# FFN 1's second GEMM on one core: difference operands and four low parts built by adding transfers, norm vectors loaded at unit 10

## The chip, the core and the metric

The kernel runs on one core of a Trainium2 chip. The metric is the device time of one execution in microseconds. Five engines work from queues of their own: PE (TensorE) multiplies, DVE (VectorE) and ACT (ScalarE) do elementwise work, POOL (GpSimd) does elementwise work and issues transfers that can add into their destination, SP (SyncE) issues plain transfers. Each queue is worked off in program order.

## The reference

One layer of a streaming encoder on 512 tokens of width 1024, all in float32. Shortened:

```
h = x + 0.5 * post1(SwiGLU_1(pre1(x)))          # FFN 1
u = pre_mix(h)                                  # RMS norm
q, k, v, xr, xg = split(u @ w_in)
...                                             # recurrent branch, attention branch, gates, w_o
h = h + post_mix(merged @ w_o)
y = h + 0.5 * post2(SwiGLU_2(pre2(h)))          # FFN 2
SwiGLU(x) = (silu(x @ w1) * (x @ w3)) @ w2      # w1, w3: 1024 x 2816, w2: 2816 x 1024
```

The change touches `@ w2` of FFN 1 (called `w2a`), the post norm and the next norm behind it, and the first products with the columns of `w_in` that are called `xr`.

## The kernel before

Every float32 operand is split in two parts of a shorter format: a high part (`whi`, a copy on ACT) and a low part (`wlo`, source minus high part). A product is three matmuls, high by high, low by high and high by low. The low part is made in one of three ways: by DVE (a subtraction; `split_to` at L179, `prep` at L649), or by an *adding transfer*: ACT writes the negative of the high part (or of the source, rounded) into the low tile, and POOL issues a transfer that adds the source onto it (`split_dma` L161, L644, L647). The low parts in the set `BY_DMA` and the products in `by_add` take the second way.

All large tiles, weights, halves and temporaries, share one ring of 42 slots (`slot`). An instruction that writes a new tile waits until the last user of the tile that held the slot before is done.

The 22 row tiles of `w2a` are multiplied in two ways. Two tiles, the *tail* (2 and 3), are multiplied plainly (`classical`, L242 to L244). The other 20 are taken in five groups (`G` = 5) by a scheme of seven products instead of eight on half tiles b11, b12, b21, b22 of 128 x 2 x 512 (`Halves`). The products come in the order m1, m5, m2, m6, m3, m7, m4, each over the five groups: 35 *units*, unit u being product u // 5 of group u % 5. m1 reads b11; m5 reads T1 = b12 - b11, which stands in b12's tile; m2 reads T2 = b22 - T1; m6 and m7 and so on read further differences or raw halves.

- `load` (L571) fetches the raw halves on SP; `prep` (L624) makes the high and low parts of one unit's weights and of its activations (`hx`, later a part of `uT`) and then, in `sums`, the differences that later units need (`T` at L582 for weights, `S` at L585 for activations), all on DVE.
- `step(u)` (L691) first preps up to unit u + 4 (`LEAD` = 5), then runs the hooks of u, then issues the 12 matmuls of unit u. So in each engine's queue a unit's preparation stands some five units ahead of its matmuls.
- `blocks` (L701) sets hooks: the tail's transfers at units 17 and 18, its split at 21 and 22, the four tiles of x (`h_back`, L711) at 20, 22, 27 and 29. The products w1, w3 before it (`pairs_a.run`) carry `late` calls: the first four units are prepped inside its last job.
- `tok_gemm` (L364) runs units 0 to 24, the tail's products for tokens 0 to 255, preps up to unit 32 (`pre.prep(5 * G + LEAD + 3)`), queues `norm(0)`, runs m7 (units 25 to 29), the tail's products for the other tokens' second half, preps the rest, queues `norm(1)`, and runs m4 twice, for one block of 128 tokens each.
- m7's sums are added out of PSUM by DVE (`out`, L682) before m4 may add into the same banks. The hooks of units 28 and 29 split the first two tiles of `xr`.
- `norm(t)` (L316) is a chain on DVE and ACT in turn: add the parts (L294), squares (L296), root, the new h (L308), squares again (L320), and the normed block hg (L331, L332). It reads two vectors spread over 128 partitions, which `vectors` (L402) loads on POOL at unit 22 (`GPOST_AT`); POOL multiplies the second one by a constant (L404). PE then transposes hg (L341), and `mm_feat` (L224 to L226) multiplies by `xr`.

Of the kernel before, what the change touches and what calls it, by code (L numbers as in the profile page):

```python
# [51 lines left out]
def hybrid_layer(ctx: ExitStack, tc: tile.TileContext, a: dict, out: bass.AP):  # L52
# [311 lines left out]
    def tok_gemm(nm, xs, n, R, gpost_name, scale, gpre_name, first, x_to=None, xf=None, spill=False, then=None, eps=None, pre=None):  # L364

        F = n - R
        acc = {}  # L370
        w = {}

        def accs(t):
            if t not in acc:
                acc[t] = [bank("acc"), bank("acc")]
            return acc[t]

        x_to = x_to or (lambda k: None)
        if not pre:
            both = min(2, F)  # L380
            for k in range(both):
                x_to(k + 1)
                w[k] = get(nm, k, ahead=both - k + 1)
            for tt in ((0, 1), (2, 3)):
                for k in range(both):
                    for t in tt:
                        mm_tok(accs(t), xs[k], t, w[k], k == 0, False)
                        if t % 2:
                            point()
            for k in range(both, F):  # L390
                x_to(k + 2)
                w[k] = get(nm, k, ahead=2 + (R - 2) * (k + 1) // F)
                for t in range(NT):
                    mm_tok(accs(t), xs[k], t, w[k], k == 0, False)
                    if t % 2:
                        point()
        point(True)
        tail = list(pre.hid.seq) if pre else list(range(F, n))
        g, us, trs = [], {}, {}
        ep = lambda t: D * EPS if eps is None else eps[:, t : t + 1]  # L400

        def vectors():  # L402
            g.extend((bcast(gpost_name), bcast(gpre_name)))
            pool.tensor_scalar(out=g[1], in0=g[1], scalar1=NEWT, scalar2=None, op0=ALU.mult)  # L404

        def tails():
            for i, k in enumerate(tail):
                x_to(F + i + 1)
                w[k] = get(nm, k, ahead=max(0, len(tail) - 1 - i), rawahead=2)

        def classical(t, n_):
            for k in tail:
                new = k == tail[0] and (t > 1 and n_ == 1 if pre else k == 0)
                mm_tok(accs(t), xs[k], t, w[k], new, k == tail[-1], (n_,), bool(pre))

        def norm(t, mid=None):
            us[t] = norms(acc[t], t, g[0], scale, g[1], spill, ep(t), mid, pre and pre.part(t), (1, 0) if pre and t > 1 else (0, 1))

        if pre:
            G = pre.G  # L420
            pre.hooks[GPOST_AT].append(vectors)
            for i in range(2):
                pre.hooks[6 * G - 2 + i].append(lambda i=i: [split_to(st["get"] + i + 1), dma_to(st["get"] + i + 3)])
            for u in range(5 * G):
                pre.step(u)
            tails()
            for t in range(2):
                acc[t] = [pre.bank["bc"][t], pre.bank["bx"][t]]
                for n_ in range(2):
                    classical(t, n_)  # L430
            pre.prep(5 * G + LEAD + 3)
            norm(0)
            for u in range(5 * G, 6 * G):
                pre.step(u)
            for t in range(2, 4):
                acc[t] = [pre.bank["bu"][t - 2], bank("acc")]
                classical(t, 1)
            pre.prep(7 * G)
            norm(1)
            for t in range(2, 4):  # L440
                for u in range(6 * G, 7 * G):
                    pre.step(u, (t - 2,))
                trs[t - 2] = transpose_mm(us[t - 2])
                transpose_out(trs[t - 2], t - 2, xf if t == 2 else None)
                classical(t, 0)
                if t == 2:
                    norm(2)
            split_to(st["get"] + len(first))
            dma_to(st["split"] + 2)
            pre.hid.eo.clear()  # L450
            pre.bank.clear()
        else:
            tails()
            vectors()
            split_to(st["get"] + len(first))
            dma_to(st["split"] + 2)
            for t in range(NT):
                for n_ in range(2):
                    classical(t, n_)
                if t == NT - 1:  # L460
                    break
                if t >= 1:
                    trs[t - 1] = transpose_mm(us[t - 1])
                if t == NT - 2:
                    transpose_out(trs[t - 1], t - 1)
                norm(t)
                if t == 1:
                    transpose_out(trs[t - 1], t - 1, xf)

        t = NT - 1  # L470
        ws, bs = [], []

        def start(ks=range(KT)):
            i = len(bs)
            ws.append(get(*first[i], ahead=len(first) - 1 - i, rawahead=2))
            bs.append(bank("f"))
# [71 lines left out]
    class Halves:  # L548
# [4 lines left out]

        names = ("m1", "m5", "m2", "m6", "m3", "m7", "m4")

        def __init__(self, nm, hid, hooks, gs, by_add, in_slots):
            self.nm, self.hid, self.hooks, self.gs = nm, hid, hooks, gs
            self.by_add, self.in_slots = by_add, in_slots
            self.G = G = len(gs)
            self.loads = [(b, i) for i in range(G) for b in ("b11", "b12")] + [(b, i) for b in ("b22", "b21") for i in range(G)]  # L560
            self.again_at = self.names.index("m3") * G - 3
            self.raw, self.ops, self.loaded, self.ready = {}, {}, 0, 0
            self.bank, self.c, self.again, self.did = {}, {}, {}, set()
# [27 lines left out]
        def t1(self, i):  # L591
            if ("t", i) not in self.did:
                self.did.add(("t", i))
                self.T("b12", "b12", "b11", i)

        def s1(self, i):
            if ("s", i) not in self.did:
# [26 lines left out]
        def prep(self, n, load=True):  # L624

            G = self.G
            while self.ready < min(n, 7 * G):
# [1 line left out]
                self.ready += 1  # L629
                m, i = self.names[u // G], u % G  # L630
                if load:
                    self.load(min(4 * G, 2 * G + (u if u >= U_SLOTS else u == 3)))
                b, odd, half = self.OPERANDS[m]
                hi = slot([P, 2, 512], F32R, name="whi")
                lo = slot([P, 2, 512], F32R, name="wlo")
# [62 lines left out]
                later(0, lambda: self.out(m), 0)  # L698
            point()

    def blocks(nm, hid, pairs, late, h_src, gs, marks, by_add, in_slots):  # L701

        hooks = {u: [] for u in range(7 * len(gs))}

# [8 lines left out]
        for at_, fn in zip(marks, (lambda n: dma_to(st["get"] + n + 1), tail_tile, h_back)):  # L713
            for n, u in enumerate(at_):
                hooks[u].append(lambda n=n, fn=fn: fn(n))
        half = Halves(nm, hid, hooks, gs, by_add, in_slots)
        pairs.more = lambda n: half.load(LOAD_PAIRS[n])
        ahead = lambda: half.prep(min(half.ready + 1, U_SLOTS))
        end = len(pairs.jobs) - 1
        late[end, 1], late[end, 2 if pairs.R is None else 3] = [ahead], [ahead]  # L720
# [6 lines left out]
        else:  # L727
            late[5, 1].append(lambda: half.s1(0))
            late[9, 1].append(lambda: half.s1(1))
            late[13, 1] = [lambda: half.s1(2)]  # L730
        pairs.run(ahead, late)
        return half

# [606 lines left out]
    late[7, 2], late[8, 2] = [lambda: softplus_terms((3, 1))], [softplus_out]  # L1340

    h.clear()
    half = blocks("w2a", hid, pairs_a, late, lambda t: a["x"][t * P : (t + 1) * P, :], GS_A, MARKS_A, ADD_A, 6 * len(GS_A))
# [423 lines left out]
    late = {(0, 1): [lambda: X2.update(t4=to_uT(tn[3], 0, 1)), tn.clear]}  # L1767
    pairs_b.prep(1, 1)

    half = blocks("w2b", hid, pairs_b, late, lambda t: h_scr[t], GS_B, MARKS_B, ADD_B, 7 * len(GS_B))  # L1770
    X2 = pairs_b = None
    last_gemm("w2b", hid, half, "ffn2_post_g", 0.5)

# [19 lines left out]
GRAW_AT = (29, 30)  # L1793
TB_AT = (34, 35, 36, 37)

BY_DMA = {("wg", i) for i in range(2)}

BY_POOL = {("wg", i) for i in range(2, 8)} | {("wk", 0), ("wk", 1)}

# [1 line left out]
KEPT_AT = (15, 16), (18, 19), (19, 20)  # L1801
LEAD = 5
U_SLOTS = 4
LOAD_PAIRS = (0, 6, 8, 10)
GS_A = (4, 6), (8, 10), (12, 14), (16, 18), (0, 20)
MARKS_A = (17, 18), (21, 22), (20, 22, 27, 29)
ADD_A = {(m, i) for m in ("m6", "m7") for i in (3, 4)} | {("m4", i) for i in range(1, 5)}

TAIL_B = (20, 21)
GS_B = (0, 2), (4, 6), (8, 10), (12, 14), (16, 18)  # L1810
# [66 lines left out]
```

## Time and profile before

| | |
|---|---|
| median of three runs | 1122.27 us (1120.18 to 1122.67) |
| the profiled execution | 1119.84 us, its span 1118.1 us |
| PE busy | 1096.8 us, 98% of the span |
| DVE, ACT, POOL busy | 942.1 us (84%), 692.3 us (62%), 398.5 us (36%) |
| DMA | 158.54 MB, mean 142 GB/s |

The span runs from the first to the last instruction of the profiled execution; what lies around it is 1.7 us. A row of a timeline gives start and duration in us, the engine, the line, the operation, its output and inputs, and in brackets the idle time before it and what ended it. Two instructions of one engine overlap a little in these rows, so their distance (the pitch), not the duration, is what one more instruction costs its queue.

### The profile page before, as it was taken

How to read it: one execution, taken by the hardware profiler on the slowest of the kernel's cores; microseconds unless marked ns; L12 is line 12 of the kernel's file. 1: busy time of each engine (PE TensorE's matmuls, PEld its weight loads, DVE VectorE, ACT ScalarE, POOL GpSimd, SP SyncE). 2: the span in 40 equal slices, each digit the busy share in tenths (PEclk: the TensorE clock that was granted, in tenths of full speed). 3: DMA queues.
4: the chain of work that ended last, by engine and by line, in shares of the span. 5: the costliest groups of instructions: out<-in, count | busy, mean ns of one | idle time of the engine just before them, and what ended most of it. 6: DMA issues, size and time to landing. Idle time of an engine off the chain costs nothing.

```text
span 1118.1 us, 18008 instructions
## 1 busy us (share of the span) xinstructions
PE 1096.8 (98%) x6826; PEld 987.2 (88%) x6826; DVE 942.1 (84%) x1335; ACT 692.3 (62%) x1200; POOL 398.5 (36%) x332
## 2 busy tenths in 40 slices
PE   9999999999979899999999999999999999999997
PEld 8899999987758777899888888888999999998886
DVE  5878999899968878878677876867789989999995
ACT  7756555577676777856565665446555555567672
POOL 0144833202021522043456564110777566521000
PEclk9999999999998999999999999999999999999999
DMA  9334653577574573126422345251433233637642
GB/s 336 117 92 128 155 120 114 174 238 144 170 219 128 172 170 111 57 69 243 140 77 94 95 170 204 75 230 57 135 110 114 82 108 94 208 133 193 184 116 92
DMA packets 53782, 158.54 MB, mean 142 GB/s; under 512 B 5552, under 2 KB 7472, under 8 KB 53696
## 3 DMA queue, kind: packets, MB, share of 16 engines
q1 hardware_dynamic: 46000, 134.81, 35.2%
q0 software_dynamic: 7408, 22.07, 10.3%
q8 instruction: 53, 0.87, 0.3%
q10 hardware_dynamic: 288, 0.52, 0.2%
q14 instruction: 33, 0.27, 0.1%
HBM read 135.37 MB, written 13.62 MB: 133 GB/s over the span
## 4 chain that ended last, share of the span: by engine, by line
PE 69%; DVE 3%; ACT 1%; issue 1%; DVEq 0%; ACTq 0%
PE f L224 8%; PE f L225 8%; PE f L226 8%; PE c L785 8%; PE c L783 8%; PE c L784 8%; PE hw L670 4%; PE hw L672 4%; PE hw L671 4%; PE acc L244 1%; PE acc L243 1%; PE acc L242 1%; PE pt L1637 1%; DVE wlo L649 1%; PE s L1601 1%
## 5 line engine op out<-in xcount | busy, mean ns | idle before, releaser
L784 PE MATMUL c<-uT,wlo 128*128 128x256 f32 x516 | 146.0, 283 | 0.0
L785 PE MATMUL c<-uT,whi 128*128 128x256 f32 x516 | 146.0, 283 | 0.0
L783 PE MATMUL c<-uT,whi 128*128 128x256 f32 x516 | 146.0, 283 | 0.0
L783 PE MATMUL c<-Xh,whi 128*128 128x256 f32 x504 | 142.7, 283 | 0.0
L784 PE MATMUL c<-Xh,wlo 128*128 128x256 f32 x504 | 142.6, 283 | 0.0
L224 PE MATMUL f<-uT,whi 128*128 128x512 f32 (+1 forms) x368 | 136.4, 371 | 0.0
L225 PE MATMUL f<-uT,wlo 128*128 128x512 f32 (+1 forms) x368 | 134.8, 366 | 0.0
L226 PE MATMUL f<-uT,whi 128*128 128x512 f32 (+1 forms) x368 | 134.8, 366 | 0.0
L785 PE MATMUL c<-Xl,whi 128*128 128x256 f32 x456 | 129.1, 283 | 0.0
L214 DVE TENSOR_TENSOR wlo<-S,whi 128x1024 fp32r<-128x1024 f32 x86 | 121.0, 1407 | 5.8 <-POOL OL L1673 3.1
L213 ACT ACTIVATE whi<-S 128x1024 fp32r<-128x1024 f32 x86 | 88.5, 1054 | 30.0 <-DVE S L832 28.3
L783 PEld LDWEIGHTS c<-uT,whi 128*128 128x128 f32 x516 | 99.0, 192 | 0.2
L784 PEld LDWEIGHTS c<-uT,wlo 128*128 128x128 f32 x516 | 99.0, 192 | 0.2
L785 PEld LDWEIGHTS c<-uT,whi 128*128 128x128 f32 x516 | 99.0, 192 | 0.0
L783 PEld LDWEIGHTS c<-Xh,whi 128*128 128x128 f32 x504 | 96.8, 192 | 0.3 <-issue 0.3
L784 PEld LDWEIGHTS c<-Xh,wlo 128*128 128x128 f32 x504 | 96.8, 192 | 0.0
L672 PE MATMUL hw<-whi,uT 128*128 128x512 f32 x228 | 89.6, 393 | 0.5
L671 PE MATMUL hw<-wlo,uT 128*128 128x512 f32 x228 | 89.3, 392 | 0.6 <-DVE wlo L649 0.3
L670 PE MATMUL hw<-whi,uT 128*128 128x512 f32 x228 | 88.8, 389 | 0.0
L785 PEld LDWEIGHTS c<-Xl,whi 128*128 128x128 f32 x456 | 87.5, 192 | 0.0
L224 PEld LDWEIGHTS f<-uT,whi 128*128 128x128 f32 x368 | 69.4, 189 | 12.5 <-issue 1.7
L226 PEld LDWEIGHTS f<-uT,whi 128*128 128x128 f32 x368 | 69.4, 189 | 11.5
(433 smaller groups left out, 3178.8 us busy)
## 6 DMA issues: line engine op xcount, KB each, us to landing
raw_w2a<-in_w2a_dram SPq DMA_DIRECT2D x27, 512.0 KB, 4.6
raw_w2b<-in_w2b_dram SPq DMA_DIRECT2D x27, 512.0 KB, 4.7
raw_w1b<-in_w1b_dram SPq DMA_DIRECT2D x22, 512.0 KB, 4.2
raw_w3b<-in_w3b_dram SPq DMA_DIRECT2D x22, 512.0 KB, 4.4
raw_w3a<-in_w3a_dram SPq DMA_DIRECT2D x21, 512.0 KB, 4.4
raw_w1a<-in_w1a_dram SPq DMA_DIRECT2D x20, 512.0 KB, 4.5
raw_wg<-in_wg_dram SPq DMA_DIRECT2D x16, 512.0 KB, 3.9
h<-in_x_dram SPq DMA_DIRECT2D x8, 512.0 KB, 6.7
```

The source lines that it names most:

```text
L213: act.activation(hi, src, AF.Copy)
L214: dve.tensor_tensor(out=lo, in0=src, in1=f32(hi), op=ALU.subtract)
L224: pe.matmul(ps[:, c0:c1], wh[:, s], h_, start=k == 0 and c0 == 0, stop=False, skip_group_check=True)
L225: pe.matmul(ps[:, c0:c1], wl[:, s], h_, start=False, stop=False, skip_group_check=True)
L226: pe.matmul(ps[:, c0:c1], wh[:, s], l_, start=False, stop=k == KT - 1, skip_group_check=True)
L242: pe.matmul(acc[n], x[:, 0, c], wh[:, s], start=first, stop=False, skip_group_check=skip)
L670: pe.matmul(ps, xs[:, 0, j, c], hi[:, j, :], start=start and j == 0, stop=False, skip_group_check=True)
L671: pe.matmul(ps, xs[:, 0, j, c], lo[:, j, :], start=False, stop=False, skip_group_check=True)
L672: pe.matmul(ps, xs[:, 1, j, c], hi[:, j, :], start=False, stop=i == self.G - 1, skip_group_check=True)
L783: pe.matmul(ps, wh[:, s], xh, start=first, stop=False, skip_group_check=True)
L784: pe.matmul(ps, wl[:, s], xh, start=False, stop=False, skip_group_check=True)
L785: pe.matmul(ps, wh[:, s], xl, start=False, stop=k == 3, skip_group_check=True)
```

## The change

- T1 of FFN 1 is no longer a subtraction on DVE. b12 isn't loaded by SP; ACT writes -b11 into a tile and POOL issues a transfer that adds b12 onto it. The first three of these are called in the last job of the products before, ahead of the units' preparation; two more are put in hooks of units 0 and 1, but `sums` calls `t1` for units 3 and 4 before those hooks run, so they come there. SP's loads are five fewer, and the calls that pace them (`LOAD_A`) are adapted. One sum of activations (`s1(3)`) is called earlier.
- The two norm vectors are loaded at unit 10 in place of 22, and ACT in place of POOL multiplies one of them, at unit 20.
- Ahead of `norm(0)` one unit less is prepped (up to 31 in place of 32).
- The low parts of both tail tiles and of the first two `xr` tiles are made by adding transfers in place of DVE.
- m4 of groups 2, 3 and 4 gets its low part from DVE in place of an adding transfer.

FFN 2 calls the same classes with the old way of T1.

```
         def vectors():
             g.extend((bcast(gpost_name), bcast(gpre_name)))
-            pool.tensor_scalar(out=g[1], in0=g[1], scalar1=NEWT, scalar2=None, op0=ALU.mult)
+            if not pre:
+                pool.tensor_scalar(out=g[1], in0=g[1], scalar1=NEWT, scalar2=None, op0=ALU.mult)
...
-            pre.hooks[GPOST_AT].append(vectors)
+            pre.hooks[2 * G].append(vectors)
+            pre.hooks[4 * G].append(lambda: act.activation(g[1], g[1], AF.Copy, scale=NEWT))
...
-            pre.prep(5 * G + LEAD + 3)
+            pre.prep(5 * G + LEAD + 2)
             norm(0)
...
-            self.loads = [(b, i) for i in range(G) for b in ("b11", "b12")] + [(b, i) for b in ("b22", "b21") for i in range(G)]
+            self.loads = [(b, i) for i in range(G) for b in (("b11",) if add_t1 else ("b11", "b12"))]
+            self.first = len(self.loads)
+            self.loads += [(b, i) for b in ("b22", "b21") for i in range(G)]
...
         def t1(self, i):
             if ("t", i) not in self.did:
                 self.did.add(("t", i))
-                self.T("b12", "b12", "b11", i)
+                if self.add_t1:
+                    t = self.raw["b12", i] = slot([P, 2, 512], name=f"raw_{self.nm}")
+                    act.activation(t, self.raw["b11", i], AF.Copy, scale=-1.0)
+                    pool.dma_start(out=t, in_=self.src("b12", i), accum_op=ALU.add)
+                else:
+                    self.T("b12", "b12", "b11", i)
...
-                    self.load(min(4 * G, 2 * G + (u if u >= U_SLOTS else u == 3)))
+                    self.load(min(self.first + 2 * G, self.first + (u if u >= U_SLOTS else u == 3)))
...
             late[13, 1] = [lambda: half.s1(2)]
+            for i in (1, 2, 3):
+                late.setdefault((end, i), []).insert(0, lambda i=i: half.t1(i - 1))
+            late[end, 1].append(lambda: half.s1(3))
+            for i in (3, 4):
+                hooks[i - 3].append(lambda i=i: half.t1(i))
...
-BY_DMA = {("wg", i) for i in range(2)}
+BY_DMA = {("wg", i) for i in range(2)} | {("w2a", i) for i in (2, 3)} | {("xr", i) for i in range(2)}
...
-LOAD_PAIRS = (0, 6, 8, 10)
+LOAD_A, LOAD_B = (0, 3, 5, 5), (0, 6, 8, 10)
...
-ADD_A = {(m, i) for m in ("m6", "m7") for i in (3, 4)} | {("m4", i) for i in range(1, 5)}
+ADD_A = {(m, i) for m in ("m6", "m7") for i in (3, 4)} | {("m4", 1)}
```

More of the change, by code (lines that the diff above doesn't have):

```diff
@@ L554, in hybrid_layer, with __init__ @@
         names = ("m1", "m5", "m2", "m6", "m3", "m7", "m4")
-        def __init__(self, nm, hid, hooks, gs, by_add, in_slots):
+        def __init__(self, nm, hid, hooks, gs, by_add, in_slots, add_t1):
             self.nm, self.hid, self.hooks, self.gs = nm, hid, hooks, gs
@@ L559, in __init__ @@
             self.G = G = len(gs)
-            self.loads = [(b, i) for i in range(G) for b in ("b11", "b12")] + [(b, i) for b in ("b22", "b21") for i in range(G)]
+            self.loads = [(b, i) for i in range(G) for b in (("b11",) if add_t1 else ("b11", "b12"))]
+            self.first = len(self.loads)
+            self.loads += [(b, i) for b in ("b22", "b21") for i in range(G)]
+            self.add_t1 = add_t1
             self.again_at = self.names.index("m3") * G - 3
@@ L699, in step, with blocks @@
             point()
-    def blocks(nm, hid, pairs, late, h_src, gs, marks, by_add, in_slots):
+    def blocks(nm, hid, pairs, late, h_src, gs, marks, by_add, in_slots, loads, add_t1=False):
         hooks = {u: [] for u in range(7 * len(gs))}
@@ L715, in blocks @@
                 hooks[u].append(lambda n=n, fn=fn: fn(n))
-        half = Halves(nm, hid, hooks, gs, by_add, in_slots)
-        pairs.more = lambda n: half.load(LOAD_PAIRS[n])
+        half = Halves(nm, hid, hooks, gs, by_add, in_slots, add_t1)
+        pairs.more = lambda n: half.load(loads[n])
         ahead = lambda: half.prep(min(half.ready + 1, U_SLOTS))
@@ L1342, in hybrid_layer @@
     h.clear()
-    half = blocks("w2a", hid, pairs_a, late, lambda t: a["x"][t * P : (t + 1) * P, :], GS_A, MARKS_A, ADD_A, 6 * len(GS_A))
+    half = blocks("w2a", hid, pairs_a, late, lambda t: a["x"][t * P : (t + 1) * P, :], GS_A, MARKS_A, ADD_A, 6 * len(GS_A), LOAD_A, True)
     X1 = pairs_a = late = None
@@ L1768, in hybrid_layer @@
     pairs_b.prep(1, 1)
-    half = blocks("w2b", hid, pairs_b, late, lambda t: h_scr[t], GS_B, MARKS_B, ADD_B, 7 * len(GS_B))
+    half = blocks("w2b", hid, pairs_b, late, lambda t: h_scr[t], GS_B, MARKS_B, ADD_B, 7 * len(GS_B), LOAD_B)
     X2 = pairs_b = None
```

## The prediction

> **What bounds the kernel now.** I read the page first, then PE's waits, then stretches of 10 us, and last the timelines of PE, DVE, ACT and POOL from 200 to 370 us, where `w2a` is. The page:
>
> ```profile
> span 1118.1 us, 18008 instructions
> PE 1096.8 (98%) x6826; PEld 987.2 (88%) x6826; DVE 942.1 (84%) x1335; ACT 692.3 (62%) x1200; POOL 398.5 (36%) x332
> ```
>
> PE has work nearly all the time and the change takes no matmul away, so it can win only what PE waits. PE's waits in the whole execution, as line waited for, us in total, times, longest:
>
> ```profile
> PE hw L670 <- DVE hc L682: 7.6, 1, 7.6
> PE tr L341 <- DVE hg L331: 3.0, 1, 3.0
> PE hw L243 <- DVE wlo L179: 1.4, 1, 1.4
> ```
>
> All three stand in the stage that is changed. Their places on PE:
>
> ```profile
> 232.31 0.40 PE L670 MATMUL hw<-whi,hx 128*128 128x512 f32 x1
> ...
> 304.52 0.39 PE L242 MATMUL hw<-whi,hT 128*128 128x512 f32 x1
> ...
> 306.94 0.50 PE L243 MATMUL hw<-wlo,hT 128*128 128x512 f32 x1 [1.36 <-DVE wlo L179]
> ...
> 325.21 0.39 PE L242 MATMUL acc<-whi,hT 128*128 128x512 f32 x1
> ...
> 327.70 0.39 PE L244 MATMUL acc<-whi,hT 128*128 128x512 f32 x1
> 335.74 0.77 PE L670 MATMUL hw<-whi,hx 128*128 128x512 f32 x1 [7.64 <-DVE hc L682]
> ...
> 340.99 0.58 PE L670 MATMUL hw<-whi,hx 128*128 128x512 f32 x1
> 341.41 0.40 PE L671 MATMUL hw<-wlo,hx 128*128 128x512 f32 x1
> 341.64 0.39 PE L672 MATMUL hw<-whi,hx 128*128 128x512 f32 x1
> ...
> 366.73 1.09 PE L341 MATMUL tr<-ident,hg 128*128 128x128 f32 x8 [3.02 <-DVE hg L331]
> ```
>
> From 325.21 to 327.70 lie 11 steps of 0.226 us, the full pace. Units 0 to 24 are 300 matmuls, 68.0 us at that pace; from 232.31 to 304.52 PE took 72.2. So 4.2 us are lost in small waits that no sum of waits shows. After the wait of 7.64 us the pitch is 0.42 (340.99 to 341.41), then 0.23: 5.5 us ran at half pace, which costs about 2.6 us more. Stretches (busy us and instructions of PE, PEld, DVE, ACT, POOL; granted clock; DMA share, GB/s):
>
> ```profile
> 230.00:240.00 10.00, 10.00 (x55) 8.69 (x54) 9.97 (x15) 4.83 (x8) 0.00 (x0) 1.00 0.85 274
> 240.00:250.00 10.00, 10.00 (x45) 8.27 (x45) 10.00 (x12) 9.34 (x14) 0.00 (x0) 1.00 0.61 203
> 330.00:340.00 10.00, 4.26 (x10) 3.42 (x11) 7.83 (x12) 7.67 (x13) 1.69 (x2) 0.56 1.03 292
> 360.00:370.00 10.00, 6.98 (x59) 6.78 (x59) 8.22 (x18) 8.51 (x21) 0.00 (x0) 1.00 0.50 169
> ```
>
> DVE has no free moment while m1 and m5 are prepped, so DVE sets the 4.2 us. The clock fell in the long wait (0.56) and didn't in the one of 3.02 us (1.00).
>
> **T1 off DVE.** First and last of the five T1, and the instruction behind the first:
>
> ```profile
> 225.55 1.22 DVE L582 TENSOR_TENSOR raw_w2a<-raw_w2a,raw_w2a 128x1024 f32<-128x1024 f32 x1
> 226.69 1.22 DVE L926 TENSOR_TENSOR cc<-cc,Rb 128x1024 f32<-128x1024 f32 x1
> ...
> 241.47 1.22 DVE L582 TENSOR_TENSOR raw_w2a<-raw_w2a,raw_w2a 128x1024 f32<-128x1024 f32 x1
> ```
>
> Each costs DVE a pitch of 1.14 us, 5.7 in all. Two stand before 230, where the ACT copies of the same units are what DVE waits for, and three added ACT copies now stand ahead of those; I count the three later ones, 3.4 us. DVE works without a gap from there on, so it reaches the tail 3.4 us sooner, and PE with it: first tail matmul at 304.5 - 3.4 = 301.1. ACT's added copies cost it 0.95 each (the pitch below) where it is busy 4.83 of 10; T1's transfers are needed 8 us or more later, and POOL is empty there (0.00). One of the three ahead of the preparation can delay a PSUM copy, and PE by some 0.3 us before 232; that and all else up to 301 is covered by what comes now.
>
> **The tail's low parts.** ACT around the second tail tile, DVE's subtraction for it, and the landing times of transfers that POOL issues to add a source in DRAM (POOL line 644 in one row, min/median/max of line 161 in the other):
>
> ```profile
> 301.17 1.04 ACT L178 ACTIVATE whi<-raw_w2a 128x1024 fp32r<-128x1024 f32 x1
> 302.12 1.04 ACT L641 ACTIVATE whi<-raw_w2a 128x1024 fp32r<-128x1024 f32 x1
> 305.67 1.22 DVE L179 TENSOR_TENSOR wlo<-raw_w2a,whi 128x1024 fp32r<-128x1024 f32 x1
> wlo<-in_w2a_dram POOLq DMA_DIRECT2D x4, 512.0 KB, 6.3
> DMA to landing us min/median/max: 4.5/6.1/9.7
> ```
>
> Before, the high part is done at 302.1 and the low part at 306.9, when PE goes on. After: 302.1 - 3.4 (DVE sooner) + 2 x 0.95 (a second ACT copy for each tail tile) = 300.6 for the negative; plus 6.3 = 306.9. So PE goes on at the same 306.9. The 3.4 us that T1 wins end up in a longer wait at the tail, in two pieces (PE can do the first tile's three matmuls in between). DVE, rid of two more subtractions, is now far ahead of PE, and ACT about 2.3 us (1.5 of the shift left, plus a wait of 0.8 on a unit-24 slot that PE now frees sooner; an estimate).
>
> The Trainium skill (DMA: Bandwidth & Descriptors, Anatomy of one DMA — SWDGE (gpsimd) path) fits such a transfer as 2.0 us plus its bytes over 436 GB/s, 3.2 us for 512 KB. By it the tail would be there at 303.8 and the change would win 3.1 us more; the rows of this trace, taken on this very queue, are twice that, and I go by them.
>
> **One unit less ahead of norm(0), vectors early.** DVE and ACT from unit 31 to the second norm:
>
> ```profile
> 315.97 0.69 DVE L214 TENSOR_TENSOR hx<-hEO,hx 128x512 fp32r<-128x512 f32 x1 [2.89 <-ACT hx L213]
> 319.46 0.69 DVE L214 TENSOR_TENSOR hx<-hEO,hx 128x512 fp32r<-128x512 f32 x1 [2.80 <-ACT hx L213]
> 320.07 0.68 DVE L294 TENSOR_TENSOR hc<-hw,hc 128x512 f32<-128x512 f32 x1
> ...
> 334.91 1.28 DVE L682 TENSOR_TENSOR hc<-hw,hc 128x512 f32<-128x512 f32 x2
> 336.93 0.68 DVE L294 TENSOR_TENSOR hc<-hw,hc 128x512 f32<-128x512 f32 x1
> ...
> 343.98 0.75 DVE L331 SCALAR_TENSOR_TENSOR hg<-h,r,bc_mix_pre_g 128x512 f32<-128x512 f32 x1
> 346.54 1.29 DVE L353 TENSOR_TENSOR uT<-tr,uT 128x512 fp32r<-128x512 f32 x2 [1.80 <-ACT uT L351]
> 347.75 0.68 DVE L294 TENSOR_TENSOR hc<-acc,hc 128x512 f32<-128x512 f32 x1
> 311.10 1.05 ACT L641 ACTIVATE whi<-raw_w2a 128x1024 fp32r<-128x1024 f32 x1
> 314.36 1.06 ACT L646 ACTIVATE wlo<-whi 128x1024 fp32r<-128x1024 f32 x1 [2.22 <-PE hw L671]
> ...
> 317.85 1.06 ACT L646 ACTIVATE wlo<-whi 128x1024 fp32r<-128x1024 f32 x1 [0.96 <-DMA wlo<-raw_w2a]
> ...
> 329.19 1.04 ACT L178 ACTIVATE whi<-raw_xr 128x1024 fp32r<-128x1024 f32 x1
> 310.38 2.78 POOL L404 TENSOR_SCALAR bc_mix_pre_g<-bc_mix_pre_g 128x1024 f32<-128x1024 f32 x1 [7.02 <-DMA bc_mix_pre_g<-in_mix_pre_g_dram]
> ```
>
> This is the heart of it. Token block 0's sums are complete some 8 matmuls behind 306.94, about 309.3, yet norm(0) starts at 320.07: in DVE's and ACT's queues it stands behind the preparation of units 30 to 32, which waits for slots. The end of the 7.64 us wait, `out(m7)` at 334.91, stands behind norm(0) and the `xr` splits. Leaving unit 32 out frees DVE at 316.6 (315.97 + 0.6), 3.5 us sooner, if unit 31 waits for its slot as before (the 2.22 us, for a matmul of unit 25, which runs at the same time as before). Without that wait the copy at 314.36 goes at 312.15 - 2.3 = 309.85, 4.5 us sooner, and norm(0) 8.0 us sooner. In between: POOL stood blocked for 7.02 + 2.78 us by the vector it scales, and the adding transfers of m7 behind it; that ends, so the slots of their sources come free some 7 us sooner. With nothing to tell which slot unit 31 gets, I take the middle, 5.75 us.
>
> Behind norm(0) the queue is longer. From 329.19 (ACT free) to 334.91 are 5.7 us. After, ACT does unit 32's copies (1.5), `xr` 0 (1.9), unit 33's high part (1.0): DVE then subtracts and splits unit 33 (1.75) and gets to `out(m7)` after 6.1. That takes 0.35 back: unit 32 and the DVE subtractions of m4 for it, against `xr`'s, which leave DVE. Unit 34's subtraction stands between `out(m7)` and norm(1), which starts 3.5 instead of 2.0 us behind. This costs nothing more: norm(1) runs 7.8 us (336.93 to 344.73) and ended 9.0 us behind PE's restart at 335.74, so it would end 10.5 behind it; with 1.3 for the transposed block's low part norm(2) starts 11.8 behind it, and before it was 12.0 (335.74 to 347.75), because DVE waited 1.80 for the transposes. If the clock stays up, PE wins 2.6 us in m4 and waits them for norm(2) and norm(3): from here the norm chain sets the end, not PE, and the 3.02 us wait at 366.73 grows instead. The `xr` transfers have over 10 us until their first matmul. The vectors' two slots for 12 units more and ACT's 1.0 for the scaling lie where ACT waits for DVE.
>
> **Sum.** -5.75 + 0.35 = -5.4 us (from -3.1 to -7.7). The profiled execution, 1118.1 of span and 1119.84 in all, would be 1114.4; it lies 2.4 below the median, 1122.27, and against that I forecast 1116.9.
>
> **Rivals.** *The tail arrives late, and the kernel is slower.* One mechanism, at the tail's second low part: line 161's longest landing is 9.7 us. Then PE goes on at 310.3, 3.4 later, and if unit 31 waits for unit 25, norm(0) gains 0.1 only. PE has then stood from 301.1 with 0.7 us of work in 9; if the clock falls as it did at 330, 2.6 us come on top: 2.5 + 0.35 slower, 1125.1. It decides from 3.1 us of lateness, with the clock fallen from 0.5. For it: the 9.7, xr's and h's loads close by. Against: the four of line 644 on the same matrix took 6.3. The Trainium skill (TensorE: Matmul & The Clock Gate, What's actually happening) has the clock halved after one idle window of about 3.4 us. The two waits in this trace agree, 7.64 with a fall and 3.02 without; by that rule the tail's wait of up to 5 us would be enough in some runs.
>
> *The slots eat the relief.* The vectors hold two of 42 slots for 12 units more, and a unit needs two: each preparation may start a unit (2.7 us) later, and of DVE's 3.4 us 0.7 are left. The tail then lands at 309.6, 2.7 late, norm(0) gains 3.5 - 2.7, less 0.35: 0.4 us, 1121.8. For it: PE and DMA releases in ACT's rows. Against: DVE, not the slot, is what came last in units 5 to 19.
>
> *The change doesn't do all it says:* the hooks for T1 of groups 3 and 4 run behind `sums`, which has called them. It costs nothing: their transfers are needed 6 us later at the earliest.
>
> **How the numbers follow.** The forecast 0.60, the late tail 0.20, the eaten slots 0.20. What a measurement can tell from no change is 0.2%, 2.2 us. Faster takes the forecast and 0.02 of the slots' spread, 0.62; same is the slots' 0.14; slower the late tail and 0.04, 0.24. The range goes from the forecast's lower end, 1114.6, less 1.1 for the runs' own spread, to 1123.5, which leaves out about half of the late tail.
>
> **What would show it.** Right: no L582 for T1, DVE idle now and then from 250 to 300, the first tail matmul near 301 and a wait for a transfer up to 307; L294 of norm(0) between 312 and 317; the wait ahead of L670 near 2.5 us in place of 7.64. Wrong: the tail's wait beyond 308, a clock below 1.00 behind it, norm(0) after 318, or the wait for L682 as long as before.

## The result, and the profile after

The changed kernel took 1117.39 us (median of 6 runs, 1115.24 to 1118.76), the kernel before 1121.06 us beside it. The ratio is 0.9964, its 95% interval 0.9951 to 0.9977: 3.7 us faster, where 5.4 were forecast. (The two profiled executions are 2.3 us apart in span: that of the kernel before was one of its fastest.) The page's span and engines, and then PE's waits:

```profile
span 1115.8 us, 18010 instructions
PE 1097.1 (98%) x6826; PEld 988.5 (89%) x6826; DVE 934.5 (84%) x1329; ACT 698.2 (63%) x1207; POOL 404.0 (36%) x337
```

```profile
PE hw L243 <- DMA wlo<-in_w2a_dram: 5.3, 2, 4.0
PE tr L341 <- DVE hg L331: 3.4, 1, 3.4
PE hw L681 <- DMA wlo<-raw_w2a: 1.0, 1, 1.0
```

DVE has lost 7.6 us of work, the span 2.3. The wait of 7.64 us for `out(m7)` (L682 before, L692 now) has gone from the list. In its place PE waits 5.3 us for the tail's low parts, which now come by transfers, and the wait ahead of the last transposes has grown from 3.0 to 3.4. The places on PE's timeline:

```profile
303.32 0.39 PE L242 MATMUL hw<-whi,hT 128*128 128x512 f32 x1
304.96 0.50 PE L243 MATMUL hw<-wlo,hT 128*128 128x512 f32 x1 [1.25 <-DMA wlo<-in_w2a_dram]
...
309.97 0.79 PE L243 MATMUL hw<-wlo,hT 128*128 128x512 f32 x1 [4.05 <-DMA wlo<-in_w2a_dram]
...
363.14 1.45 PE L341 MATMUL tr<-ident,hg 128*128 128x128 f32 x8 [3.39 <-DVE hg L331]
```

The tail starts 1.2 us sooner than before (304.52), but its second low part lets PE go on at 309.97, 3.0 later than before (306.94). The last transposes come 3.6 us sooner (363.14 for 366.73). Stretches of the changed kernel, columns as in the prediction:

```profile
280.00:290.00 10.00, 9.02 (x40) 7.11 (x39) 10.00 (x14) 6.36 (x11) 0.00 (x0) 1.00 1.01 290
...
310.00:320.00 10.00, 10.00 (x32) 8.00 (x33) 5.53 (x9) 5.56 (x10) 0.85 (x1) 0.70 0.86 179
330.00:340.00 10.00, 10.00 (x46) 8.28 (x45) 9.21 (x16) 5.67 (x11) 0.86 (x1) 1.00 0.80 166
360.00:370.00 10.00, 6.86 (x45) 6.86 (x46) 7.20 (x12) 8.85 (x17) 3.14 (x2) 0.83 0.86 319
```

From 330 to 340 PE is now busy throughout at full clock, where before it stood for more than half. The clock has fallen behind the tail's wait instead (0.70) and behind the wait at the end (0.83; 1.00 before). The row of 280 to 290 shows DVE without a free moment still, and the DMA engines full. The other engines at the places that the prediction named:

```profile
301.54 1.04 ACT L160 ACTIVATE wlo<-raw_w2a 128x1024 fp32r<-128x1024 f32 x1
302.87 0.86 POOL L161 DMA_DIRECT2D wlo<-in_w2a_dram  x1 [4.05 <-ACT wlo L160]
313.75 1.06 ACT L656 ACTIVATE wlo<-whi 128x1024 fp32r<-128x1024 f32 x1 [2.19 <-DMA wlo<-raw_w2a]
315.97 0.68 DVE L294 TENSOR_TENSOR hc<-hw,hc 128x512 f32<-128x512 f32 x1
331.20 1.28 DVE L692 TENSOR_TENSOR hc<-hw,hc 128x512 f32<-128x512 f32 x2
344.14 0.68 DVE L294 TENSOR_TENSOR hc<-acc,hc 128x512 f32<-128x512 f32 x1
```

`norm(0)` starts at 315.97, 4.1 us sooner than before; `out(m7)` 3.7 and `norm(2)` 3.6 sooner.

### The profile page after: what moved, and what is told of

Same layout as the page of the kernel before. It is cut to its first block, busy times and chain, and to the rows that moved or that the text cites. A ratio compares the mean times of both kernels' runs of the same rounds, so it can differ in the third digit from the quotient of the medians.

```text
span 1115.8 us, 18010 instructions
## 1 busy us (share of the span) xinstructions
PE 1097.1 (98%) x6826; PEld 988.5 (89%) x6826; DVE 934.5 (84%) x1329; ACT 698.2 (63%) x1207; POOL 404.0 (36%) x337
## 4 chain that ended last, share of the span: by engine, by line
PE 88%; ACT 4%; issue 3%; DMA 3%; DVE 2%; POOL 0%; DVEq 0%; SPq 0%; POOLq 0%; ACTq 0%
PE c L798 13%; PE c L800 13%; PE c L799 13%; PE f L224 9%; PE f L225 9%; PE f L226 9%; PE hw L681 4%; PE hw L680 3%; PE hw L682 3%; PE acc L242 1%; PE acc L244 1%; PE acc L243 1%; DMA wlo<-raw_w2a 1%; PE pt L1652 1%; DMA wlo<-in_w2a_dram 1%
## 5 line engine op out<-in xcount | busy, mean ns | idle before, releaser
L682 PE MATMUL hw<-whi,uT 128*128 128x512 f32 x228 | 88.9, 390 | 0.0
```

The costliest lines, as they stand in the source:

```text
L682: pe.matmul(ps, xs[:, 1, j, c], hi[:, j, :], start=False, stop=i == self.G - 1, skip_group_check=True)
```

## What the experiments are compared by

Each kernel ran beside the kernel before, and the difference is taken from that. The two last columns are from its profile: the first L294 of `norm(0)`, and the way from there to the first L294 of `norm(2)`. "Undone" kernels are the change without one part, "alone" kernels are the kernel before with one part.

| kernel | us | before beside it | difference | 95% interval of the ratio | `norm(0)` | to `norm(2)` |
|---|---|---|---|---|---|---|
| before | | | | | 320.07 | 27.7 |
| the change | 1117.39 | 1121.06 | -3.7 | 0.9951 to 0.9977 | 315.97 | 28.2 |
| vectors undone | 1122.47 | 1120.45 | +2.0 | 1.0007 to 1.0024 | 320.41 | 28.2 |
| unit 32 undone | 1117.03 | 1120.45 | -3.4 | 0.9953 to 0.998 | 317.11 | 26.9 |
| T1 undone | 1119.97 | 1120.45 | -0.5 | 0.9985 to 1.0002 | 317.54 | 28.2 |
| tails undone | 1113.25 | 1120.45 | -7.2 | 0.9916 to 0.9943 | 313.39 | 28.1 |
| m4 undone | 1124.63 | 1121.36 | +3.3 | 1.002 to 1.0041 | 315.48 | 35.8 |
| xr undone | 1117.69 | 1121.36 | -3.7 | 0.9956 to 0.9977 | 315.20 | 28.4 |
| m4 and xr undone | 1117.80 | 1120.53 | -2.7 | 0.9965 to 0.9982 | 315.41 | 28.9 |
| vectors alone | 1117.33 | 1121.36 | -4.0 | 0.9952 to 0.9977 | 317.56 | 27.7 |
| T1 alone | 1118.17 | 1120.53 | -2.4 | 0.9961 to 0.9981 | 318.41 | 27.6 |
| tails alone | 1127.37 | 1121.36 | +6.0 | 1.0043 to 1.0068 | 327.91 | 27.6 |
| tails undone, xr later | 1111.02 | 1120.53 | -9.5 | 0.9902 to 0.993 | 311.63 | 26.1 |
| and the fourth xr tile later | 1110.08 | 1121.07 | -11.0 | 0.989 to 0.9919 | 311.76 | 26.1 |

But for m4 undone, and for the last two, which shorten it, the way from `norm(0)` to `norm(2)` is 26.9 to 28.9 us whatever else is changed: the start of `norm(0)` carries most of the result, as the prediction had it, to within 2 us.

Two things limit what the table can tell. The intervals reach 1.0 to 1.6 us to either side, so two rows differ for certain only from some 2 us on. And a profile is one execution: the change and four of its variants (unit 32, m4, xr, m4 and xr undone) have the same instructions up to the tail, yet their first tail matmuls lie at 303.32, 301.78, 301.31, 301.38 and 301.60. In the profile of tails undone the whole stage starts some 1.7 us late (first matmul of unit 0 at 234.04; 231.9 to 232.6 in all others), ahead of everything that differs in it.

The question was which part moves that start: the POOL queue that the early vectors free, unit 32, or DVE's relief by T1, and whether the tails' transfers cost. Each expectation spells out its theories; a letter means what that expectation says.

## One part undone

**The vectors** loaded at unit 22 and scaled by POOL again:

```
-            pre.hooks[2 * G].append(vectors)
-            pre.hooks[4 * G].append(lambda: act.activation(g[1], g[1], AF.Copy, scale=NEWT))
+            pre.hooks[GPOST_AT].append(vectors)
```

> The change with the norm vectors loaded at unit 22 and scaled by POOL again. Theory A (POOL blocked behind the vector holds m7's adding transfers and so the slot that unit 31 waits for): these are issued near 313 in place of 306.4 and 308.9, unit 31's low copy starts 3 to 7 us later than 313.75, 1119 to 1123. Theory B (the vectors' early slots cost as much as the blocked POOL): within 1 us of the change.

The whole gain goes, and 2 us more. POOL's and DVE's rows of this kernel:

```profile
311.33 2.77 POOL L404 TENSOR_SCALAR bc_mix_pre_g<-bc_mix_pre_g 128x1024 f32<-128x1024 f32 x1 [9.19 <-DMA bc_mix_pre_g<-in_mix_pre_g_dram]
314.17 1.82 POOL L655 DMA_DIRECT2D wlo<-raw_w2a  x2
319.80 0.69 DVE L214 TENSOR_TENSOR hx<-hEO,hx 128x512 fp32r<-128x512 f32 x1 [10.53 <-ACT hx L213]
```

POOL stands 9.19 us for the vector that it is to scale, and two adding transfers of m7 stand behind it till 314.17. DVE, in the preparation behind them, stands idle for 10.53 us, and the next in its queue is `norm(0)`. In the kernel before, m7's first two transfers were issued at 313.22 in the same way; in the change, with POOL free, from 306.38 on:

```profile
313.22 1.82 POOL L647 DMA_DIRECT2D wlo<-raw_w2a  x2
```

```profile
306.38 0.85 POOL L657 DMA_DIRECT2D wlo<-raw_w2a  x1 [2.65 <-ACT wlo L656]
308.93 0.85 POOL L657 DMA_DIRECT2D wlo<-raw_w2a  x1 [1.70 <-ACT wlo L656]
```

This run takes back both halves of the part, the early load and the scaling on ACT; which of the two is enough by itself was not tried.

**Unit 32** prepped ahead of `norm(0)` again (`LEAD + 3`):

> The change with unit 32 prepped ahead of norm(0) again. Theory A (norm(0)'s start sets the end): norm(0) starts 3 to 4 us later, near 319.5, out(m7) about 3 us later, a wait ahead of m4 of 1 to 2 us comes back; 3 us slower than the change, near 1120.5. Theory B (PE sets the end since the tail): less than 1 us slower.

The time is the change's. The rows of `norm(0)`, `out(m7)` and `norm(2)`, to be held against 315.97, 331.20 and 344.14:

```profile
317.11 0.68 DVE L294 TENSOR_TENSOR hc<-hw,hc 128x512 f32<-128x512 f32 x1
...
331.05 1.28 DVE L692 TENSOR_TENSOR hc<-hw,hc 128x512 f32<-128x512 f32 x2
...
343.99 0.68 DVE L294 TENSOR_TENSOR hc<-acc,hc 128x512 f32<-128x512 f32 x1
```

`norm(0)` comes 1.1 us later (1.6 to 1.9 later than with m4, xr or both undone, where the tail started at about the same time) and `out(m7)` 0.15 sooner. The unit's preparation only moves from the near to the far side of `norm(0)`, both ahead of `out(m7)`.

**T1** on DVE again (the old loads and calls):

> The change with T1 back on DVE and b12 loaded by SP. Theory A (DVE's 3.4 us are handed on to norm(0) through ACT and DVE queues): the tail starts near 304.5, its second low part lands near 312 to 314, norm(0) starts 2 to 3.5 us later than 315.97; 1119.5 to 1121. Theory B (what T1 wins is lost in the tail's wait): within 0.7 us of the change, 1117 to 1118.

3.2 us of the 3.7 go. The tail starts at 304.14 and its second low part lets PE go on at 312.63, as theory A had it; `norm(0)` comes 1.6 later, less than its 2 to 3.5, and `norm(2)` 1.6 later (345.70). In spans the two profiles are 1.9 us apart, so the size is 2 to 3 us.

**The tails** on DVE again:

```
-BY_DMA = {("wg", i) for i in range(2)} | {("w2a", i) for i in (2, 3)} | {("xr", i) for i in range(2)}
+BY_DMA = {("wg", i) for i in range(2)} | {("xr", i) for i in range(2)}
```

> The change with the two tail tiles' low parts back on DVE. Theory A (the norm chain behind norm(0) sets the end, the tail's wait for its transfers is mostly hidden behind it): PE starts the tail near 302.6 and goes through without the 1.6 and 4.5 us waits and without the half clock, but then waits some 5 us for out(m7); norm(0) starts 1 to 2 us sooner than 315.97, since ACT has two copies less; 1 to 2 us faster than the change, 1115.5 to 1116.5. Theory B (the tail's waits set the end): the 3.0 us of lateness and the 2.6 us of half clock come back, 1111 to 1113. Theory C (DVE needs the relief): PE waits for DVE at the tail as before, 1118 to 1120.

The gain doubles, from 3.7 to 7.2 us. PE's longest wait in this kernel:

```profile
PE hw L680 <- DVE hc L692: 3.5, 1, 3.5
```

No wait is left at the tail; PE is far enough ahead to wait 3.5 us for `out(m7)` again, and still `norm(2)` starts 2.6 us sooner than in the change, in a profile whose stage began late. So of the change's parts this one costs, by some 3.5 us.

**m4 and xr.** In the change, m4 of groups 2 to 4 gives up its adding transfers and xr takes two. Undone one at a time:

```
+ADD_A = {(m, i) for m in ("m6", "m7") for i in (3, 4)} | {("m4", i) for i in range(1, 5)}
```

> The changed kernel with one part undone: the low parts of m4's groups 1 to 4 are made by adding transfers again, where the change leaves only group 1 to them. Theory A (this part of the change is worth nothing: the other parts make up its 3.7 us between them): within 1 us of the change. Rival (DVE sets the norm chain from 316 to 360, three subtractions of 1.2 us leave it): norm(2) comes 2 to 3.5 us sooner than 344.14 and the kernel is 2 to 3.5 us faster than the change. Rival (the transfers crowd the DMA engines, which are busy 0.8 to 0.9 of this stage): low parts of m4 land late, PE waits for them, and the kernel is 1 to 4 us slower.

```
+BY_DMA = {("wg", i) for i in range(2)} | {("w2a", i) for i in (2, 3)}
```

> The changed kernel with one part undone: the low parts of the first two tiles of xr are made by DVE again, not by adding transfers. Theory A (this part is worth nothing, for the same reason): within 1 us of the change. Rival (the two subtractions of 1.2 us stand between norm(0) and out(m7) in DVE's queue, and the norm chain sets the end): out(m7)'s L692 at 333.6 in place of 331.20, norm(2) 2.4 us later, the kernel 2 to 2.5 us slower than the change.

m4 alone undone was 7.0 us slower than the change, by the mechanism of the last rival but beyond its 4 us; xr undone was no different. POOL and PE with m4 undone, and then a stretch:

```profile
326.95 0.86 POOL L657 DMA_DIRECT2D wlo<-raw_w2a  x1 [11.49 <-ACT wlo L656]
329.36 0.86 POOL L161 DMA_DIRECT2D wlo<-in_xr_dram  x1 [1.56 <-ACT wlo L160]
331.40 0.86 POOL L657 DMA_DIRECT2D wlo<-raw_w2a  x1 [1.18 <-ACT wlo L656]
333.81 0.86 POOL L161 DMA_DIRECT2D wlo<-in_xr_dram  x1 [1.55 <-ACT wlo L160]
335.86 0.86 POOL L657 DMA_DIRECT2D wlo<-raw_w2a  x1 [1.18 <-ACT wlo L656]
340.77 0.80 PE L681 MATMUL hw<-wlo,hx 128*128 128x512 f32 x1 [3.12 <-DMA wlo<-raw_w2a]
345.75 0.79 PE L681 MATMUL hw<-wlo,hx 128*128 128x512 f32 x1 [2.05 <-DMA wlo<-raw_w2a]
```

```profile
340.00:350.00 10.00, 7.18 (x20) 5.50 (x21) 4.27 (x12) 3.10 (x9) 0.00 (x0) 0.50 0.60 146
```

m4's transfers now alternate with xr's, and PE, which needs m4's before xr's, waits for three of them (6.1 us in all; the two longest are shown) with its clock at half (0.50). Whether it was the two together was tried by undoing both:

> The changed kernel with the low parts of m4's groups 1 to 4 by adding transfers again and those of xr by DVE again, both as before. The changed kernel with m4 alone undone was 7 us slower than the change, xr alone undone the same. Theory E (the cut of m4's transfers only makes room for xr's: both together in ACT's and POOL's queues between norm(0) and m4 are what makes m4's low parts late): no wait for m4's low parts of 1 us or more, and the time within 1.5 us of the change. Rival F (m4's own transfers are late behind a tail that comes 3 us late): PE waits 2 us or more for low parts in m4, the clock falls there, and the kernel is 4 to 8 us slower than the change.

Within 1.0 us of the change, with at most 0.9 us of a single wait for m4's low parts: without xr's transfers between them they land nearly in time. The two parts are an exchange that is worth about 1 us, which the intervals don't tell from nothing; m4's half of it is what makes room for xr's.

## One part alone

**The vectors alone** in the kernel before:

> The kernel before with one part of the change alone: the norm vectors are loaded at unit 10 and scaled by ACT at unit 20, so POOL no longer stands behind a vector that is still under way. Theory A (the blocked POOL queue is what held norm(0); some 5 us of the change's gain are here): norm(0)'s first L294 comes 3 to 6 us sooner than 320.07, between 314 and 317, and the kernel takes 4 to 6 us less than before, 1114.5 to 1116.5. Theory B (the prediction: unit 32 ahead of norm(0) holds 3.5 us, the POOL queue 2.3): 1.5 to 3 us less, 1117.5 to 1119. Rival C (the early vectors hold two slots that the preparation of m1 and m5 wants): the first tail matmul comes later than 304.5 by 1 us or more, and the time is within 1 us of before.

By the medians all of the change's gain is there, 4.0 us, between theories A and B. Its `norm(0)` and its longest wait:

```profile
317.56 0.68 DVE L294 TENSOR_TENSOR hc<-hw,hc 128x512 f32<-128x512 f32 x1
```

```profile
PE hw L672 <- DVE hc L684: 5.2, 1, 5.2
```

`norm(0)` comes 2.5 us sooner, less than theory A's 3 to 6 and close to the 2.3 that theory B gave to POOL's queue: the tail (306.87) is where it was, and the wait of 7.64 us went to 5.2. The profiled span is 2.6 us shorter (1115.5 for 1118.1).

**T1 alone:**

> The kernel before with one part of the change alone: the five T1 are made by a negative copy on ACT and an adding transfer, and the loads of b12 go. Theory A (DVE is what PE waits for up to the tail, and norm(0) follows the tail): first tail matmul 2 to 3.5 us sooner than 304.5, norm(0) 2 to 3 us sooner than 320.07, the kernel 2 to 3 us faster than before, 1118.4 to 1119.4. Rival D (the vector under way in POOL's queue sets norm(0) by itself): the tail comes sooner, norm(0) stays within 1 us of 320.07 and the time within 1 us of before.

2.4 us faster. PE, POOL and `norm(0)`:

```profile
300.87 0.39 PE L242 MATMUL hw<-whi,hT 128*128 128x512 f32 x1
308.58 2.95 POOL L404 TENSOR_SCALAR bc_mix_pre_g<-bc_mix_pre_g 128x1024 f32<-128x1024 f32 x1 [8.88 <-DMA bc_mix_pre_g<-in_mix_pre_g_dram]
311.59 2.70 POOL L655 DMA_DIRECT2D wlo<-raw_w2a  x3
318.41 0.68 DVE L294 TENSOR_TENSOR hc<-hw,hc 128x512 f32<-128x512 f32 x1
```

The tail starts 3.65 us sooner, and `norm(0)` 1.7, which neither theory had. It goes with POOL, which issues m7's transfers 1.6 sooner (311.59 for 313.22), and not with the tail: Rival D's mechanism, with the vector itself issued sooner (298.61 for 302.26).

**The tails alone:**

> The kernel before with one part of the change alone: the low parts of the two tail tiles are made by a negative copy on ACT and an adding transfer. Theory A (this part costs): the second low part lands 7 us behind ACT's negative, which ends at 304, so PE goes on at about 311 in place of 306.9; norm(0) comes 2 us or more later than 320.07 and the kernel takes 2 to 5 us more than before, 1122.5 to 1125.5. Theory B (the prediction: the tail's lateness is covered by DVE's 2.4 us less of work): within 1 us of before. Rival C (the tail's own lateness is hidden since norm(0) waits for the blocked POOL queue anyway): PE goes on at 311 but norm(0) stays within 1 us of 320.07, and the time within 1 us of before, since the wait of 7.64 us ahead of out(m7) shrinks by what the tail takes.

6 us slower, above the 2 to 5 of theory A. PE, POOL and DVE:

```profile
304.89 0.87 POOL L281 DMA_DIRECT2D bc_ffn_post_g<-in_ffn_post_g_dram  x1
...
313.51 0.79 PE L243 MATMUL hw<-wlo,hT 128*128 128x512 f32 x1 [6.55 <-DMA wlo<-in_w2a_dram]
316.07 2.77 POOL L404 TENSOR_SCALAR bc_mix_pre_g<-bc_mix_pre_g 128x1024 f32<-128x1024 f32 x1 [9.78 <-DMA bc_mix_pre_g<-in_mix_pre_g_dram]
324.74 0.69 DVE L214 TENSOR_TENSOR hx<-hEO,hx 128x512 fp32r<-128x512 f32 x1 [11.31 <-ACT hx L213]
```

The tail's own lateness is 6.6 us (306.94 to 313.51). Here the vectors are loaded late still, and now behind the tail's transfers in POOL's queue (304.89 for 302.26): POOL comes to its multiplication 5.7 us later than before, and `norm(0)` comes 7.8 us later. With the vectors early the same part cost 3.5 us. So the parts don't add up singly, but in this order they nearly do: vectors and T1, 4.0 + 2.4 = 6.4 faster alone, against 7.2 for the change without the tails; then the tails' 3.5 back, which leaves the 3.7 of the change. Vectors and T1 as a pair were not run, so that sum is argued and not shown.

## Two steps further

In the change without the tails, DVE's `out(m7)` (328.60) stood behind the preparation of units 32 and 33, and that behind ACT's four copies for xr, which stood ahead of unit 33's and unit 34's high parts. The copies were moved behind unit 34's preparation:

```
-                pre.hooks[6 * G - 2 + i].append(lambda i=i: [split_to(st["get"] + i + 1), dma_to(st["get"] + i + 3)])
...
             pre.prep(7 * G)
+            for i in range(2):
+                split_to(st["get"] + i + 1)
+                dma_to(st["get"] + i + 3)
             norm(1)
```

> The changed kernel with the tails' low parts on DVE (which ran at 1113.25) and, on top of that, the two xr tiles split not at units 28 and 29 but behind the preparation of unit 34, just ahead of norm(1): four ACT copies of 0.95 us leave the way from norm(0) to out(m7). Theory A (ACT's copies for the preparation of units 33 and 34 are what out(m7) stands behind, 328.60, while PE had m7 done at 325.9): out(m7) at about 326, the wait of 3.52 us ahead of m4 goes to 0.5 or less, the clock stays up in m4, norm(2) 2 to 4 us sooner, and the kernel takes 1109 to 1111.5 us. Rival (the copies now delay norm(1)'s first pass on ACT, and what m4 wins is waited for the norm chain): the wait ahead of m4 goes, the wait for L331 ahead of the transposes grows by as much, and the time is within 1 us of 1113.25.

1111.02 us, 2.2 less by the medians (the two intervals overlap a little). PE's waits of this kernel, and then three of DVE's rows:

```profile
PE tr L341 <- DVE hg L331: 3.4, 1, 3.4
PE hw L681 <- DVE hc L693: 1.6, 1, 1.6
```

```profile
325.22 1.28 DVE L693 TENSOR_TENSOR hc<-hw,hc 128x512 f32<-128x512 f32 x2
...
347.01 2.36 DVE L179 TENSOR_TENSOR wlo<-raw_xr,whi 128x1024 fp32r<-128x1024 f32 x2
349.29 0.68 DVE L294 TENSOR_TENSOR hc<-acc,hc 128x512 f32<-128x512 f32 x1
```

`out(m7)` is at 325.22; of the wait of 3.5 us 1.6 are left, more than theory A's 0.5. `norm(2)` comes 3.8 us sooner (337.71), but `norm(0)` already 1.8, since the profile of tails undone began its stage late; what the move itself gives is the shorter way between them, 26.1 for 28.1 us. The last two rows show the next place of the same kind: two xr tiles are split in front of `norm(3)`, whose sums PE had finished at 344.4. One of the two was moved behind it:

> The kernel of the run before (tails on DVE, two xr tiles split ahead of norm(1); 1111.02) with the fourth xr tile split behind norm(3) and not in front of it: one ACT copy of 1.0 and one DVE subtraction of 1.2 us leave the queue ahead of norm(3)'s L294, which stood there at 349.29 while its sums had been done at 344.4. Theory A (DVE's and ACT's queue order sets the start of norm(3), and the wait of 3.40 us ahead of the last transposes is what lets the clock fall there): L294 at about 348.1, the wait at the transposes 2.0 to 2.5 us, no fall of the clock behind it (pitch of the matmuls 0.12 in place of 0.21), and 1.5 to 3 us less: 1108 to 1109.5. Rival (the chain is bound elsewhere, by ACT's squares or by the tile that now comes late): the wait stays above 3 us or a new one stands ahead of xr's fourth tile, and the time is within 1 us of 1111.

The transposes of this kernel, and a stretch, here and in the kernel before this one:

```profile
355.71 1.09 PE L341 MATMUL tr<-ident,hg 128*128 128x128 f32 x8 [2.26 <-DVE hg L331]
```

```profile
350.00:360.00 10.00, 7.74 (x66) 7.54 (x66) 7.32 (x16) 8.54 (x20) 0.95 (x1) 1.00 0.66 230
```

```profile
350.00:360.00 10.00, 6.61 (x44) 6.40 (x43) 8.28 (x18) 7.82 (x19) 0.00 (x0) 0.77 0.53 172
```

The wait went from 3.40 to 2.26 and the clock stays at 1.00, as theory A expected. In the profiles the span is 3.5 us shorter (1106.8 for 1110.3), but the one is the fastest execution of its kernel and the other one of the slower ones. The medians differ by 0.9 only, outside theory A's time and within the rival's 1 us, and the ratios' intervals overlap, so its size in time isn't settled. This kernel, 1110.08 us, is the fastest of all: 11 us under the kernel before, against 3.7 for the change.

## Why the prediction was near, point by point

**The sum.** 5.75 were forecast for `norm(0)` and 4.1 came; 0.35 to be given back behind it, and 0.5 were (28.2 for 27.7). The end wait grew, but by 0.4 us, where the prediction left room for up to 2.6. What was not in the sum is the clock at the end: of the 3.6 us by which the last transposes came sooner the span kept 2.3. The other profiles settle where the 1.3 went. From the start of the last transposes to the end of the span the six executions whose clock stays up behind them (the kernel before, the three parts alone, unit 32 undone and the last kernel) take 751.1 to 751.4 us; the eight whose clock falls there take 752.6 to 753.6, the change 752.7. The prediction has no term for this: it put the price of the clock behind the last wait at nothing, as it was behind the 3.02 us.

**The cause of the 5.75 was wrong.** The prediction gave 3.5 us to leaving out unit 32, if unit 31 waits as before, and the rest, up to 8.0, to POOL's release. The runs put it the other way round:

| part | `norm(0)`, undone | `norm(0)`, alone | time, undone | time, alone |
|---|---|---|---|---|
| vectors (POOL's release) | 4.4 | 2.5 | 5.7 | 4.0 |
| T1 | 1.6 | 1.7 | 3.2 | 2.4 |
| unit 32 | 1.1 to 1.9 | not run | 0.3 or nothing | not run |
| tails | -2.6 | -7.8 | -3.5 | -6.0 |

(What the part wins, in us; below zero, what it costs.) The step that failed is that leaving unit 32 out frees DVE 3.5 us sooner: it freed `norm(0)` by 1.1 to 1.9, and what is put off stands in the same two queues ahead of `out(m7)`, so that nothing of it reaches the time. The prediction priced that at 0.35 without asking what the shift was then worth. The upper bound, with its row of 7.02 + 2.78 us on POOL, held the true cause: POOL issues m7's transfers some 7 us sooner, as it said.

**T1** was right for itself: 3.4 us sooner at the first tail matmul were forecast, and 3.65 came with T1 alone. That DVE sets the 4.2 us lost ahead of the tail was right too. From the first matmul of unit 0 to the tail PE took 72.2 us in the four profiles with T1 on DVE, and 68.3, nearly the 68.0 of the full pace, in the two with T1 off DVE and the vectors late. With the vectors early it took 69.1 to 69.6 in seven kernels, and 71.1 in the profile of the change. So the 1.2 us by which the tail came sooner in that profile are low by chance: 0.75 of what is lacking are waits for three of m2's adding transfers, between 262 and 270 us, that the kernels with the same instructions don't have. The early vectors cost about 1 us of T1's gain, as a wait for an adding transfer of m6 (0.98 at 287.07; 1.20 with unit 32 undone). It is less than the 2.7 of the rival of the eaten slots, and that slots cause it is not shown. DVE had next to no idle moment from 250 to 290 and some from 290 to 300 (9.33 of 10 us busy), so that sign was half right.

**The tail.** The prediction had PE go on at 300.6 + 6.3 = 306.9. ACT's negative ended at 302.6, 2.0 later than forecast, in a profile whose tail itself was 2.2 later than forecast, and from the transfer's issue to the matmul it took 7.1 us (302.87 to 309.97). So 3.0 late, and with the fall (12 steps at 0.43 in place of 0.23, and one at each end in between) 2.8 more: the mechanism of the rival of the late tail, in full, and two of the signs that were to prove the prediction wrong. In the four kernels with the same instructions PE went on at 308.5 to 309.3, 1.6 to 2.4 late, and the clock fell there too. (The row that the prediction took the 9.7 us from, line 161, is of transfers at 386 to 401 us, none of them of `w2a`.) The late tail did not make the kernel slower because the rival's second condition failed: unit 31 did not wait for a matmul of unit 25 but for a transfer of m7 (the 2.19 us), and that transfer came off a free POOL queue. Undoing it shows what it cost, 3.5 us.

The prediction set the Trainium skill's figure (DMA: Bandwidth & Descriptors, Anatomy of one DMA — SWDGE (gpsimd) path; by its fit an estimate of 3.2 us for 512 KB) aside for the row of 6.3 us. The changed kernel's DMA issues bear that out, and go further (last number: median us from issue to landing):

```profile
wlo<-in_w2a_dram POOLq DMA_DIRECT2D x6, 512.0 KB, 7.2
raw_w2a<-in_w2a_dram POOLq DMA_DIRECT2D x5, 512.0 KB, 9.4
raw_w2a<-in_w2a_dram SPq DMA_DIRECT2D x22, 512.0 KB, 7.3
```

**The wait ahead of `out(m7)`**, forecast at 2.5, was nil: PE came there late by the tail's 3.0 and 2.8 us. That right and wrong met at 1117 is luck: a gain under-sized (POOL), one that never reached the time (unit 32) and a cost that was put with a rival (the tail) happened to cancel.

## What to carry to other kernels

An elementwise instruction that waits for a transfer, in a queue that also issues transfers, held everything behind it; load its operand long before and do the work on an engine that issues none (here both were done at once). An adding transfer in place of a subtraction won time where its consumer was farther away than the landing under load (T1; the medians here were 7.2 and 9.4 us); just ahead of its matmul (the tails) it cost more than the subtraction that it saved. Putting work from before a chain to behind it is no gain while it stays ahead of the same consumer: ask which instruction in the queue is needed first, and put copies that nobody needs yet behind it.

## What the hardware showed

- Beside more adding transfers, and with the DMA engines full (1.01 in the row of 280 to 290), plain loads of `w2a` on SP took 7.3 us from issue to landing in the median. In the ten kernels with T1's transfers the median is 6.3 to 7.3, in the four without 4.5 to 5.0; the first lack T1's five loads and issue the others at other times, so the cause of the difference isn't taken apart. On the page of before the same loads have this row:

```profile
raw_w2a<-in_w2a_dram SPq DMA_DIRECT2D x27, 512.0 KB, 4.6
```

- From the tail on, the clock was at half behind every wait of PE of 3.38 us or more, or fell within 1.5 us of it (the matmuls' pitch doubles, 0.43 for 0.23 us or 0.21 for 0.12). Behind shorter waits it went both ways. It stayed up behind 2.26 us and behind 3.02, 3.03, 3.03 and 3.04 (the last transposes of the last kernel, the kernel before and the three parts alone). It fell behind 2.98 (the tail, T1 undone), 3.01 and 3.12 (the last transposes and m4, with m4 undone), and with unit 32 undone 2 us behind a wait of 1.59. So the length of one wait does not decide it. The Trainium skill (TensorE: Matmul & The Clock Gate, What's actually happening) puts the idle window at about 3.4 us, and says that it runs free, so that runs of one kernel differ. The waits of about 3 us that went both ways agree with a window that runs free; the falls behind waits shorter than 3.4 us do not agree with one whole window without work, and there the measurement decides. What counts as idle no run here shows.
